# Linear attention: loads a group ahead and its two parts a group apart; two buffers for transposed cached keys

## The chip, the cores and the metric

The kernel runs on one core of a Trainium2 chip. The metric is the device time of one execution in microseconds. The instructions of each engine (PE is the matrix engine, DVE the vector engine, ACT the scalar engine, POOL is GpSimd, SP issues DMAs) form one list that the engine works off in order, and semaphores hold an instruction back until what it needs is there.

## What is computed

One layer of a decoder for 1024 prompt tokens and 8 sequences of 8 sample tokens (1088 rows). After an input projection, half of the mixing width is gated linear attention and half is latent attention, for the sample tokens over a paged cache of 8192 keys a sequence. Then come an output projection and a gated convolutional feed-forward net. The parts that matter here:

```python
def step(S, inp):                     # linear attention, one chunk of 64 tokens, 4 heads
    qc, kc, vc, gc = inp
    b = jnp.cumsum(gc, axis=1)
    o_inter = jnp.einsum('bchk,bhkv->bchv', qc * jnp.exp(b), S)
    diff = jnp.where(tri, b[:, :, None] - b[:, None, :], -jnp.inf)
    att = jnp.einsum('bthk,bshk,btshk->bhts', qc, kc, jnp.exp(diff))
    o_intra = jnp.einsum('bhts,bshv->bthv', att, vc)
    bl = b[:, -1]
    S_new = S * jnp.exp(bl)[..., None] + jnp.einsum('bshk,bshv->bhkv', kc * jnp.exp(bl[:, None] - b), vc)
    return S_new, o_inter + o_intra
...
s = jnp.einsum('bthl,bsl->bhts', ql, kv) + jnp.einsum('bthr,bsr->bhts', qr, kr)   # latent attention
p = jax.nn.softmax(jnp.where(k_pos[None, :] <= qp[:, None], s * scale, -jnp.inf))
return jnp.einsum('bhts,bsl->bthl', p, kv)
```

## The kernel before

All products are in fp32 (or in two rounded parts). The kernel is written in a tile framework: program text gives instructions and their rank, and a scheduler builds each engine's list from that rank, a modelled clock and the buffers that are free. Tiles live in pools; a tag with one buffer lets the next tile of that tag start only when every reader of the last one has finished, and a pool that is closed hands its space to the pool that follows with the same kind of waits.

After phase 1 (norm, input projection) two generators run side by side, `interleave` choosing by the work that each `yield` reports. One is `mla_sample`: for 8 sequences and 4 pieces of 2048 keys each it gathers rows (`L`, `R`) with POOL's indirect DMAs, transposes them on PE into `kps` (L1176), copies them with ACT into `KT` and `KR` (L1178), takes scores `S` (L1186, L1188), a running softmax (L1191 to L1215) and sums `O` (L1220). `KT` and `KR` have one buffer each; `kps` has two. Its rank is set 450 behind the other's, so it fills what the other leaves free.

The other, `main`, goes through the prompt's queries, `gla` (linear attention), `mla_prompt` (the prompt's latent attention) and the loads of the output weights. `gla` takes five groups: 4 is the sample tokens, 0 to 3 are 256 prompt tokens each. `gla_group` does one group from loads to store. Its first part depends on no other group: loads of `qT`, `kT`, `v`, `la` (L609 to L615), running sums `bps` and `bT` (L620, L623), seven levels of scores `lps` written into `att` (L630 to L679; each level is e on POOL and DVE, its exponential on ACT, products `Ab` and `Bb` on DVE, 16 small matmuls), decayed queries and keys `qe`, `ek`, `ke`, `dec` (L683 to L700). Its second part carries the state `S`: four chunk steps of `ops` (L716, L723), `ups` (L808) and the update of `S` and `Sb` (L728 to L735), or `gla_sample` for group 4, then norm, gate (L746) and the store (L747). `v`, `la`, `bT`, `att`, `qe`, `ek`, `ke` and `dec` have one buffer. Group 4 has a pool of its own, "glas", which is closed before "gla" opens for the others:

```python
with self.pool("glas") as bp:
    yield from self.gla_group(G, cp, bp, pm, 4)
with self.pool("gla") as bp:
    for g in range(4):
        yield from self.gla_group(G, cp, bp, pm, g)
```

Of the kernel before, what the change touches and what calls it, by code (L numbers as in the profile page):

```python
# [10 lines left out]
F32 = mybir.dt.float32  # L11
# [4 lines left out]
ALU = mybir.AluOpType  # L16
AX = mybir.AxisListType
PSUM = bass.MemoryType.PSUM
DRAM = bass.MemoryType.DRAM

P = 128
# [18 lines left out]
def _consts():  # L40
    c = {}
    r = RO
# [22 lines left out]
    # the rows of a modulation: four parts of nine in steps of 32, then the bias  # L65
# [28 lines left out]
class Rows:  # L94
    """the transposes of all tokens' rows, in two parts each, by groups of tokens"""
# [10 lines left out]
class Kernel:  # L106
# [37 lines left out]
    def mm2(self, out, w, ws, start, stop):  # L144
        """sums over ws of products, 64 rows in w: their first parts, then their second ones; the sums of the
        result's two halves are what counts"""
        n = len(ws)
        for k in range(n):
            for j in range(2):
                self.nc.tensor.matmul(out, w[:, k], ws[k][j], start=start and k + j == 0, stop=stop and k + j == n)  # L150

    def halves(self, pool, ps, tag="rt", bufs=2):
        """the sums of rows r and 64 + r"""
        o = pool.tile([P, T if tag == "big" else D], F32, name=tag, tag=tag, bufs=bufs)[0:64, 0:ps.shape[1]]
        self.nc.vector.tensor_copy(o, ps[64:P])
        self.nc.vector.tensor_tensor(o, ps[0:64], o, ALU.add)
        return o

    def rstd(self, pool, ms, n, tag="rstd", ms2=None):
        p = ms.shape[0]  # L160
        t = pool.tile([P, n], F32, name=tag + "e", tag=tag + "e")
        r = pool.tile([P, n], F32, name=tag, tag=tag)
# [72 lines left out]
    def ada_section(self, sec, wp, pp, bufs, evac, rp=None):  # L235
# [9 lines left out]
                # four products side by side  # L245
# [60 lines left out]
    def gate(self, k, gvec, gp, name, gb):  # L306
        """gate rows times the norm's gain, for prompt and sample tokens: [128, 2, 1024]"""
# [18 lines left out]
    def to_T(self, xp, pp, xn, h, i, slot, nraw=3, eng=None, both=None):  # L326
        """xn: the normalized rows of tile i; their transposes, modulated, into h"""
# [24 lines left out]
    def phase1(self):  # L352
# [3 lines left out]
        with ExitStack() as es:  # L356
# [37 lines left out]
            # the sample tokens' two parts side by side  # L394
# [22 lines left out]
            def gates():  # L417
                """the forget gates"""
# [18 lines left out]
            def ada():  # L437
                """the other parts of the modulation, a little after each of the products"""
# [19 lines left out]
            # low-rank gate input and query latent  # L458
# [20 lines left out]
            # latents and rotary keys  # L479
# [24 lines left out]
            # GLA queries and keys, transposed  # L504
# [19 lines left out]
            # indices of the sixteenths of pages, by partition  # L524
# [8 lines left out]
            # values and output gates  # L533
# [18 lines left out]
    def rope(self, xp, out, x, tab, h):  # L552
        """out, x: [n, h, 64]; tab [n, 2, 64]"""
# [13 lines left out]
    def gla(self):  # L567
        nc, A = self.nc, self.A
        with ExitStack() as es:
# [26 lines left out]
    def gla_group(self, G, cp, bp, pm, g):  # L596
        nc, A = self.nc, self.A
        sample = g == 4
        t0 = g * 256
        n = 64 if sample else 256  # L600
        nt = 1 if sample else 2
        nch = n // 64
        m = min(n, P)
        blk = 8 if sample else 64
        fl = lambda x: x[:, 0:2 * n].rearrange("p (a t) -> p a t", a=2)
        flat = lambda name, bufs=1: fl(bp.tile([P, 2 * n], F32, name=name, tag=name, bufs=bufs))
        rows = lambda name, bufs=1: bp.tile([P, nt, 512], F32, name=name, tag=name, bufs=bufs)[0:m]
        qT, kT = flat("qT", 2), flat("kT", 2)
        nc.sync.dma_start(qT, self.s_qk[0:2, :, t0:t0 + n].rearrange("c p t -> p c t"))  # L609
        nc.sync.dma_start(kT, self.s_qk[2:4, :, t0:t0 + n].rearrange("c p t -> p c t"))  # L610
# [14 lines left out]
        # intra-block scores, by levels  # L625
        # odd blocks of 64 on the upper partitions, where their values are
        npar, rows_ = (1, 64) if sample else (2, P)
        att = bp.tile([P, 2 * nt, P], F32, name="att", tag="att")[0:rows_]
        nc.gpsimd.memset(att, 0.0)
        for li, L in enumerate(LEVELS):  # L630
# [11 lines left out]
            else:  # L642
                G.flip ^= 1
                X = 2 * n // (2 * L)
# [3 lines left out]
                ref = b2[:, :, L - 1:L].broadcast_to([P, X, L])  # L648
# [44 lines left out]
        dec = bp.tile([P, 16], F32, name="dec", tag="dec")[:, 0:2 * nb].rearrange("p (a c) -> p a c", a=2)  # L693
# [5 lines left out]
        ke = bp.tile([P, nt, 2, P], F32, name="ke", tag="ke")[0:m]  # L699
# [3 lines left out]
        o_sb = rows("o_sb")  # L703
# [39 lines left out]
        rg = rows("rg")  # L743
        nc.sync.dma_start(rg, self.s_r[t0:t0 + n].rearrange("(i p) d -> p i d", p=m))
        self.head_norm(bp, o_sb, m, nt * 4)
# [4 lines left out]
    def head_norm(self, bp, o, m, nh, gg=None):  # L750
# [3 lines left out]
        sq = bp.tile([P, nh, P], F32, name="hsq", tag="hsq", bufs=1)[0:m]  # L754
# [3 lines left out]
        rs = self.rstd(bp, ms, nh, "hrs")  # L758
# [4 lines left out]
    def gla_sample(self, cp, pm, qe, ke, dec, v, at2, o_sb):  # L763
# [17 lines left out]
        for b in range(8):  # L781
            Sb = Sbs[b % 2]
            for h in range(2):
                hr = slice(64 * h, 64 * h + 64)
                nc.scalar.copy(Sb[hr, :, h], Sall[hr, b])
# [5 lines left out]
            self.outer(ups, lambda p, h: km[:, b, p * P + 64 * h:p * P + 64 * h + 64], v[:, 0])  # L791
            nc.gpsimd.tensor_tensor(Sall[:, b], Sall[:, b], dec[:, :, b:b + 1].broadcast_to([P, 2, P]), ALU.mult)
            nc.vector.tensor_tensor(Sall[:, b], ups, Sall[:, b], ALU.add)
            nc.sync.dma_start(A["o_gla_s"][0, b].rearrange("(p h) k v -> (h k) p v", h=2), Sall[:, b])
# [8 lines left out]
    def outer(self, out, k, v):  # L803
        """the heads' sums of keys times values, two heads side by side"""
# [15 lines left out]
    def mla_weights(self, mp, pp):  # L820
# [5 lines left out]
        # the first head's first  # L826
# [77 lines left out]
    def sample_queries(self, zs, xs, ds, es2):  # L904
        """the sample tokens' queries, and the prompt's last ones"""
# [24 lines left out]
            # the last tokens: those of the prompt, then the sample tokens  # L930
# [23 lines left out]
    def prompt_queries(self):  # L954
        """the prompt's other queries, and the attention among the new tokens"""
# [13 lines left out]
    def mix(self, gen, side, ratio, chain=None):  # L969
        """run gen, and side by its side in proportion, and a step of chain after each of gen's; what gen returns"""  # L970
# [12 lines left out]
    def mla_prompt(self):  # L983
        nc, A = self.nc, self.A
        with ExitStack() as es:
# [23 lines left out]
            def split2(x, name):  # L1009
                """both parts of [128, 2, n]"""  # L1010
# [6 lines left out]
            def keys(h):  # L1017
                """a head's keys, transposed"""
# [14 lines left out]
            def vals(pr):  # L1033
                """a pair of heads' values"""
# [14 lines left out]
            def scores(h, m):  # L1049
# [3 lines left out]
                # the rotary queries, twice: their first parts, then their second ones  # L1053
# [43 lines left out]
            def values(h, m, ps_, ls):  # L1097
# [3 lines left out]
                for j0 in range(0, end, 2):  # L1101
                    # the last block is the second tile's only
# [622 lines left out]
```

## Time and profile before

| what | us |
|---|---|
| median of three runs | 1891.44 (1888.42 to 1892.9) |
| span of the profiled execution | 1894.2 |
| PE busy in it | 1815.7 (96%) |
| DVE, ACT, POOL busy in it | 939.5, 709.2, 527.4 |

The profiled execution is one of its own, recorded by its span alone, from the first to the last instruction. Linear attention runs from about 400 to 640 us of the span, beside pieces of the sample attention, which itself lasts from about 333 to 960 us. Busy shares are of the span. A PE that is busy may still run at half of its clock; PEclk, the granted clock, says when.

### The profile page before, as it was taken

The page shows a single profiled execution, that of the slowest core. Times are in us where ns is not written, and L with a number is a line of the kernel's source. Part 1 is how long each engine was busy: PE and PEld are TensorE (multiplying, and loading weights), DVE is VectorE, ACT ScalarE, POOL GpSimd, SP SyncE. Part 2 cuts the span into 40 slices and gives each one's busy share as a digit, 9 for nine tenths or more (in the row PEclk, how much of TensorE's full clock was granted, in tenths as well). Part 3 has the DMA queues.
Part 4 walks back from the last instruction along what each step waited for, and adds up shares of the span by engine and source line. Part 5 has one row for each costly group of instructions (what it writes and reads, how often), then busy time and mean ns, then how long its engine had stood idle before and what let it go on. Part 6 is the DMA issues. An engine that isn't in the chain of part 4 may idle for free.

```text
span 1894.2 us, 30775 instructions
## 1 busy us (share of the span) xinstructions
PE 1815.7 (96%) x12403; PEld 1502.5 (79%) x12403; DVE 939.5 (50%) x1680; ACT 709.2 (37%) x1398; POOL 527.4 (28%) x567
## 2 busy tenths in 40 slices
PE   6999999998998899999999999999999999999998
PEld 3888767764555567776679999999999999888787
DVE  4740334355676445554557755555555554623433
ACT  3451112464456556756633422222222222323322
POOL 2640101243334323232102123333333332202221
PEclk8999999999989999999999999999999999999999
DMA  8155553565454744545445331111121212744563
GB/s 312 68 171 180 187 160 111 192 206 180 169 183 159 250 160 150 188 138 180 159 145 176 101 98 68 61 64 63 68 70 69 70 62 70 246 115 114 155 188 94
DMA packets 170617, 265.26 MB, mean 140 GB/s; under 512 B 18277, under 2 KB 118693, under 8 KB 162282
## 3 DMA queue, kind: packets, MB, share of 16 engines
q1 hardware_dynamic: 156138, 179.39, 29.6%
q0 software_dynamic: 14336, 83.89, 12.7%
q8 instruction: 98, 1.61, 0.3%
q14 instruction: 45, 0.37, 0.1%
HBM read 221.49 MB, written 41.75 MB: 139 GB/s over the span
## 4 chain that ended last, share of the span: by engine, by line
PE 83%; DVE 6%; DMA 5%; ACT 3%; issue 2%; POOL 1%; SPq 1%; DVEq 0%; POOLq 0%; ACTq 0%
PE ups L140 9%; PE ups L142 9%; PE ups L141 9%; PE kps L1176 6%; PE yps L142 4%; PE yps L140 4%; PE yps L141 4%; PE zps L140 3%; PE O L1220 3%; PE zps L142 3%; PE zps L141 3%; PE S L1186 3%; PE y L142 2%; PE y L140 2%; PE y L141 2%
## 5 line engine op out<-in xcount | busy, mean ns | idle before, releaser
L140 PE MATMUL ups<-gh,uhi 128*128 128x384 f32 (+1 forms) x1056 | 347.2, 329 | 0.3 <-DVE hraw L343 0.3
L141 PE MATMUL ups<-gl,uhi 128*128 128x384 f32 (+1 forms) x1056 | 346.7, 328 | 0.0
L142 PE MATMUL ups<-gh,ulo 128*128 128x384 f32 (+1 forms) x1056 | 346.5, 328 | 0.0
L1514 DVE TENSOR_SCALAR cv<-u,vt 128x1024 f32<-128x1024 f32 (+1 forms) x88 | 133.2, 1534 | 216.3 <-ACT u L1504 179.4
L140 PEld LDWEIGHTS ups<-gh,uhi 128*128 128x128 f32 x1056 | 198.3, 188 | 0.7 <-DVE hraw L343 0.6
L142 PEld LDWEIGHTS ups<-gh,ulo 128*128 128x128 f32 x1056 | 198.3, 188 | 0.1
L141 PEld LDWEIGHTS ups<-gl,uhi 128*128 128x128 f32 x1056 | 198.3, 188 | 0.0
L1176 PE MATMUL kps<-ident,L 128*128 128x128 f32 x1024 | 159.9, 286 | 22.4 <-ACT KT L1178 16.2
L1178 ACT COPY KT<-kps 128x512 f32<-128x512 f32 x256 | 145.8, 590 | 82.8 <-PE kps L1176 77.5
L1176 PEld LDWEIGHTS kps<-ident,L 128*128 128x128 f32 x1024 | 113.8, 143 | 78.8 <-issue 42.5
L121 POOL TENSOR_TENSOR ulo<-uraw,uhi 128x2048 fp32r<-128x2048 f32 x24 | 111.4, 4642 | 207.5 <-ACT uhi L1342 204.6
L1504 ACT COPY u<-ups 128x384 f32<-128x384 f32 (+1 forms) x130 | 57.6, 444 | 279.2 <-PE ups L142 279.2
L142 PE MATMUL yps<-uhi,gl 128*128 128x512 f32 x341 | 133.3, 392 | 5.0 <-DVE gl L121 5.0
L140 PE MATMUL yps<-uhi,gh 128*128 128x512 f32 x341 | 133.1, 391 | 0.0
L141 PE MATMUL yps<-ulo,gh 128*128 128x512 f32 x341 | 133.0, 390 | 0.0
L121 DVE TENSOR_TENSOR gl<-graw,gh 128x1408 fp32r<-128x1408 f32 x31 | 59.1, 1908 | 129.3 <-ACT gh L1561 129.3
L1167 POOL DMA_INDIRECT R<-cache_krope,idx x64 | 66.1, 1033 | 181.6 <-PE kps L1176 148.5
L1342 ACT CAST uhi<-uraw 128x2048 fp32r<-128x2048 f32 (+1 forms) x38 | 70.8, 1865 | 94.4 <-PE ups L141 66.9
L1561 ACT CAST gh<-graw 128x1408 fp32r<-128x1408 f32 (+1 forms) x35 | 45.8, 1310 | 158.1 <-PE yps L141 128.6
L1166 POOL DMA_INDIRECT L<-cache_latent,idx x64 | 61.5, 961 | 138.9 <-PE O L1220 68.4
L140 PE MATMUL zps<-whi,hh 128*128 128x512 f32 (+2 forms) x256 | 96.1, 375 | 0.0
L142 PE MATMUL zps<-whi,hl 128*128 128x512 f32 (+2 forms) x256 | 94.2, 368 | 0.8 <-DVE hl L121 0.8
(443 smaller groups left out, 3799.1 us busy)
## 6 DMA issues: line engine op xcount, KB each, us to landing
wraw<-w_ada SPq DMA_DIRECT2D x48, 512.0 KB
uraw<-w_ffn_up SPq DMA_DIRECT2D x22, 1024.0 KB
graw<-s_g SPq DMA_DIRECT2D x32, 704.0 KB
s_g<-gl SPq DMA_DIRECT2D x22, 544.0 KB
uraw<-w_ffn_down SPq DMA_DIRECT2D x10, 1024.0 KB
xt<-x_prompt SPq DMA_DIRECT2D x16, 512.0 KB
wraw<-w_in SPq DMA_DIRECT2D x12, 512.0 KB
uraw<-w_o SPq DMA_DIRECT2D x4, 1024.0 KB
```

What stands on the lines that cost most here:

```text
L121: eng.tensor_tensor(out, x, hi.bitcast(F32), ALU.subtract)
L140: mm(out, wh, xh, start=start, stop=False)
L141: mm(out, wh, xl, start=False, stop=False)
L142: mm(out, wl, xh, start=False, stop=stop)
L1166: nc.gpsimd.indirect_dma_start(L.rearrange("p j l -> p (j l)"), None, cl, io)
L1167: nc.gpsimd.indirect_dma_start(R.rearrange("p j l -> p (j l)"), None, ck, io)
L1176: nc.tensor.transpose(ps[:, k], x, self.ident)
L1178: nc.scalar.copy(KT[:, q // 2, j0:j0 + 4] if q < 4 else KR[:, 4 * half:4 * half + 4], ps)
L1186: nc.tensor.matmul(S[r], Q[:, c], KT[:, c, :, r], start=(c == 0), stop=False)
L1342: self.nc.scalar.copy(hi, raw)
L1504: copy(u[:, 2 + c0:2 + c0 + m], ps[:, 0:m])
L1514: nc.vector.tensor_scalar(yv[z], sh(2)[z], self.cw2[:, ch:ch + 1], self.cb[:, ch:ch + 1], ALU.mult, ALU.add)
```

## The change

`gla_group` is cut in three. `gla_load` allocates and loads `qT`, `kT` and `la`, and is called one group ahead of the first part. `gla_intra` is the first part, `gla_inter` the second. A group's `gla_inter` runs next to the following group's `gla_intra` through `beside`, which picks by work done as `interleave` does. Both pools are open together: "gla" holds everything that groups share, sized for the prompt's groups, "glas" only what the sample group needs. `v`, `la`, `att`, `qe`, `ke` and `dec` get two buffers. In `gla_sample` the masked keys are made one sequence at a time (three buffers in place of eight parts), the states are loaded four ahead into five buffers in place of eight, and there is a `yield` after each sequence in place of one for all. `KT` and `KR` get two buffers. Comments are dropped throughout.

```diff
-            with self.pool("glas") as bp:
-                yield from self.gla_group(G, cp, bp, pm, 4)
-            with self.pool("gla") as bp:
-                for g in range(4):
-                    yield from self.gla_group(G, cp, bp, pm, g)
+            bp = es.enter_context(self.pool("gla"))
+            order = (4, 0, 1, 2, 3)
+            with self.pool("glas") as sp:
+                ahead = self.gla_load(bp, 4)
+                for n, g in enumerate(order):
+                    X, ahead = ahead, self.gla_load(bp, order[n + 1]) if n < 4 else None
+                    intra = self.gla_intra(G, bp, pm, X)
+                    if n == 0:
+                        yield from intra
+                    else:
+                        yield from self.beside((inter, 15.0 if n == 1 else 11.4), (intra, 10.3))
+                    if n == 1:
+                        break
+                    inter = self.gla_inter(G, bp, sp, pm, X)
+            for n in (2, 3, 4):
+                inter = self.gla_inter(G, bp, None, pm, X)
+                X, ahead = ahead, self.gla_load(bp, order[n + 1]) if n < 4 else None
+                yield from self.beside((inter, 11.4), (self.gla_intra(G, bp, pm, X), 10.3))
+            yield from self.gla_inter(G, bp, None, pm, X)
+
+    def beside(self, *gens):
+        live = [[0.0, total, g] for g, total in gens]
+        while live:
+            it = min(live, key=lambda x: x[0] / x[1])
+            try:
+                c = next(it[2])
+                it[0] += c
+            except StopIteration:
+                live.remove(it)
+                continue
+            yield c
+
+    def gla_load(self, bp, g):
...
+        X.qT, X.kT = X.flat("qT", 2), X.flat("kT", 2)
+        nc.sync.dma_start(X.qT, self.s_qk[0:2, :, t0:t0 + n].rearrange("c p t -> p c t"))
+        nc.sync.dma_start(X.kT, self.s_qk[2:4, :, t0:t0 + n].rearrange("c p t -> p c t"))
+        X.la = bp.tile([P, 2, 256], F32, name="la", tag="la", bufs=2)[0:m, 0:nt]
+        nc.sync.dma_start(X.la, self.s_la[t0:t0 + n].rearrange("(i p) k -> p i k", p=m))
+        return X
+
+    def gla_intra(self, G, bp, pm, X):
...
-        v = rows("v")
+        X.v = v = X.rows("v", 2)
         nc.sync.dma_start(v, self.s_v[t0:t0 + n].rearrange("(i p) d -> p i d", p=m))
-        la = bp.tile([P, nt, 256], F32, name="la", tag="la")[0:m]
-        nc.sync.dma_start(la, self.s_la[t0:t0 + n].rearrange("(i p) k -> p i k", p=m))
...
-        att = bp.tile([P, 2 * nt, P], F32, name="att", tag="att")[0:rows_]
+        X.att = att = bp.tile([P, 4, P], F32, name="att", tag="att", bufs=2)[0:rows_, 0:2 * nt]
...
-        qe = flat("qe")
+        X.qe = qe = flat("qe", 2)
...
+    def gla_inter(self, G, bp, sp, pm, X):
...
-            self.gla_sample(bp, pm, qe, ke, dec, v, att, o_sb)
-            yield 15.0
+            yield from self.gla_sample(sp, pm, qe, ke, dec, v, att, o_sb)
...
-        km = cp.tile([64, 8, 256], F32, name="km")
-        for b in range(8):
-            nc.scalar.mul(km[:, b], ke[:, 0].rearrange("p a k -> p (a k)"), self.small[0:64, 96 + b:97 + b])
...
-        Sall = cp.tile([P, 8, 2, P], F32, name="Sall")
-        for b in range(8):
-            nc.sync.dma_start(Sall[:, b], A["state_gla"][0, b].rearrange("(p h) k v -> (h k) p v", h=2))
+        def load(b):
+            Ss.append(cp.tile([P, 2, P], F32, name="Sall", tag="Sall", bufs=5))
+            nc.sync.dma_start(Ss[b], A["state_gla"][0, b].rearrange("(p h) k v -> (h k) p v", h=2))
+        for b in range(4):
+            load(b)
...
+            if b < 4:
+                load(b + 4)
+            km = cp.tile([64, 256], F32, name="km", tag="km", bufs=3)
+            nc.scalar.mul(km, ke[:, 0].rearrange("p a k -> p (a k)"), self.small[0:64, 96 + b:97 + b])
...
+            yield 1.8
...
-                        KT = bp.tile([P, 2, 16, P], F32, name="KT", tag="KT", bufs=1)
-                        KR = bp.tile([P, 8, P], F32, name="KR", tag="KR", bufs=1)
+                        KT = bp.tile([P, 2, 16, P], F32, name="KT", tag="KT", bufs=2)
+                        KR = bp.tile([P, 8, P], F32, name="KR", tag="KR", bufs=2)
```

## Rows read from the trace of the kernel before

**Rows 1.** The page: PE's busy tenths and granted clock in 40 slices of 47 us.

```profile
PE   6999999998998899999999999999999999999998
...
PEclk8999999999989999999999999999999999999999
```

**Rows 2.** Windows by stage: busy us (instructions) by engine, granted clock, DMA share, GB/s.

```profile
330.00:400.00 70.00, 66.53 (x571) 50.87 (x570) 25.76 (x87) 32.66 (x67) 21.07 (x20) 1.00 0.53 191
400.00:640.00 240.00, 213.70 (x2224) 133.32 (x2228) 149.02 (x382) 134.69 (x292) 95.64 (x105) 0.95 0.55 185
640.00:960.00 320.00, 306.90 (x2627) 214.24 (x2616) 165.89 (x474) 194.12 (x468) 81.91 (x107) 0.99 0.51 170
...
1060.00:1620.00 560.00, 559.65 (x3457) 556.53 (x3456) 301.34 (x335) 140.68 (x239) 179.92 (x180) 1.00 0.21 73
```

**Rows 3.** Windows of 20 us in linear attention, columns PE, PEld, DVE, ACT, POOL, clock.

```profile
440.00:460.00 20.00, 12.68 (x135) 8.14 (x128) 7.58 (x20) 6.53 (x13) 4.77 (x6) 0.84 0.71 253
...
500.00:520.00 20.00, 18.07 (x203) 12.43 (x206) 12.89 (x37) 9.20 (x20) 5.41 (x7) 0.83 0.38 110
...
540.00:560.00 20.00, 16.93 (x184) 12.35 (x182) 16.22 (x37) 8.66 (x17) 6.22 (x6) 0.74 0.26 83
...
580.00:600.00 20.00, 15.98 (x183) 9.73 (x181) 19.62 (x44) 13.13 (x28) 11.54 (x12) 1.00 0.44 145
```

**Rows 4.** Waits of PE, 400 to 640 us: total us, times, longest.

```profile
PE kps L1176 <- ACT KT L1178: 11.1, 11, 7.0
PE lps L669 <- DVE Bb L662: 8.4, 5, 3.1
```

**Rows 5.** Timeline of the first prompt group's start: start us, duration, instruction.

```profile
437.87 0.37 SPq L609 DMA_DIRECT2D qT<-s_qk  x1
...
454.25 0.88 DVE L641 COPY B<-qT 64x512 f32<-64x512 f32 x2 [8.65 <-DMA qT<-s_qk]
...
456.83 1.11 PE L1176 MATMUL kps<-ident,L 128*128 128x128 f32 x4 [6.99 <-ACT KT L1178]
```

**Rows 6.** Waits of POOL, 400 to 640 us.

```profile
POOL att L629 <- PE ops L716: 20.4, 3, 8.4
```

**Rows 7.** Timeline of the second prompt group's start.

```profile
498.15 2.35 POOL L746 TENSOR_TENSOR o_sb<-o_sb,rg 128x1024 f32<-128x1024 f32 x1 [1.77 <-DVE o_sb L759]
498.51 2.27 DVE L650 TENSOR_TENSOR e<-bT 128x256 f32<-128x256 f32 x1
...
501.93 1.12 PE L669 MATMUL lps<-Bb,Ab 128*64 128x64 f32 x16 [2.70 <-DVE Bb L662]
```

**Rows 8.** Tile e, 400 to 640 us: duration in ns, shortest, median, longest.

```profile
L650 DVE TENSOR_TENSOR e<-bT x27: 229/424/2573, 406.6 to 596.2; 128x256 f32<-128x256 f32 x24, 128x64 f32<-128x64 f32 x3
```

**Rows 9.** Groups of POOL instructions, 400 to 640 us: busy us, mean ns.

```profile
L649 POOL TENSOR_TENSOR e<-bT 128x256 f32<-128x256 f32 (+1 forms) x27 | 17.5, 656 | 27.0 <-ACT KT L1178 10.1 <-DVE Bb L662 9.1 <-ACT bT L623 6.1
...
L746 POOL TENSOR_TENSOR o_sb<-o_sb,rg 128x1024 f32<-128x1024 f32 (+1 forms) x5 | 10.8, 2164 | 6.5 <-DVE o_sb L759 6.4
```

**Rows 10.** Waits of PE, 640 to 960 us.

```profile
PE kps L1176 <- ACT KT L1178: 4.2, 5, 2.3
```

**Rows 11.** Timeline: transposes of keys, four in a run and eight in a run.

```profile
495.17 0.66 PE L1176 MATMUL kps<-ident,L 128*128 128x128 f32 x4
...
498.15 1.09 PE L1176 MATMUL kps<-ident,L 128*128 128x128 f32 x8
```

**Rows 12.** Window of 5 us while the sample group loads.

```profile
405.00:410.00 5.00, 5.00 (x38) 2.58 (x38) 3.21 (x13) 4.17 (x13) 2.83 (x6) 1.00 0.98 350
```

**Rows 13.** Timeline of the end of the sample attention.

```profile
949.60 1.05 PE L1188 MATMUL S<-KR,Qd 128*32 128x256 f32 x16
...
953.25 0.91 SPq L1368 DMA_DIRECT2D mx<-s_mix  x2
```

**Rows 14.** Waits of ACT, 400 to 640 us.

```profile
ACT e L651 <- DVE e L650: 20.4, 10, 6.9
```

More of the change, by code (lines that the diff above doesn't have):

```diff
@@ L157, in halves, with rstd @@
         return o
-    def rstd(self, pool, ms, n, tag="rstd", ms2=None):
+    def rstd(self, pool, ms, n, tag="rstd", ms2=None, full=False):
         p = ms.shape[0]
-        t = pool.tile([P, n], F32, name=tag + "e", tag=tag + "e")
-        r = pool.tile([P, n], F32, name=tag, tag=tag)
+        t, r = (pool.tile([P, 8 if full else n], F32, name=x, tag=x)[:, 0:n] for x in (tag + "e", tag))
         if ms2 is None:
@@ L589, in gla @@
             G.flip = 0
-            with self.pool("glas") as bp:
-                yield from self.gla_group(G, cp, bp, pm, 4)
-            with self.pool("gla") as bp:
-                for g in range(4):
-                    yield from self.gla_group(G, cp, bp, pm, g)
[L596 to L601, printed above, removed]
+            bp = es.enter_context(self.pool("gla"))
@@ new lines, in gla_load @@
+    def gla_load(self, bp, g):
+        nc = self.nc
+        X = type("X", (), {})()
+        X.g, X.sample = g, g == 4
+        X.t0 = t0 = g * 256
+        X.n = n = 64 if X.sample else 256
+        X.nt = nt = 1 if X.sample else 2
+        X.m = m = min(n, P)
+        X.fl = lambda x: x[:, 0:2 * n].rearrange("p (a t) -> p a t", a=2)
+        X.flat = lambda name, bufs=1: X.fl(bp.tile([P, 512], F32, name=name, tag=name, bufs=bufs))
+        X.rows = lambda name, bufs=1: bp.tile([P, 2, 512], F32, name=name, tag=name, bufs=bufs)[0:m, 0:nt]
+        X.qT, X.kT = X.flat("qT", 2), X.flat("kT", 2)
[4 more added lines that the diff above has]
+        return X
@@ L602, in gla_group @@
+    def gla_intra(self, G, bp, pm, X):
+        nc = self.nc
+        sample, n, nt, m, t0, qT, kT, la, flat, fl = X.sample, X.n, X.nt, X.m, X.t0, X.qT, X.kT, X.la, X.flat, X.fl
         nch = n // 64
-        m = min(n, P)
         blk = 8 if sample else 64
-        fl = lambda x: x[:, 0:2 * n].rearrange("p (a t) -> p a t", a=2)
-        flat = lambda name, bufs=1: fl(bp.tile([P, 2 * n], F32, name=name, tag=name, bufs=bufs))
-        rows = lambda name, bufs=1: bp.tile([P, nt, 512], F32, name=name, tag=name, bufs=bufs)[0:m]
@@ L608, in gla_group @@
-        qT, kT = flat("qT", 2), flat("kT", 2)
-        nc.sync.dma_start(qT, self.s_qk[0:2, :, t0:t0 + n].rearrange("c p t -> p c t"))
-        nc.sync.dma_start(kT, self.s_qk[2:4, :, t0:t0 + n].rearrange("c p t -> p c t"))
-        v = rows("v")
+        X.v = v = X.rows("v", 2)
         nc.sync.dma_start(v, self.s_v[t0:t0 + n].rearrange("(i p) d -> p i d", p=m))
-        la = bp.tile([P, nt, 256], F32, name="la", tag="la")[0:m]
-        nc.sync.dma_start(la, self.s_la[t0:t0 + n].rearrange("(i p) k -> p i k", p=m))
@@ L643, in gla_group @@
                 G.flip ^= 1
-                X = 2 * n // (2 * L)
+                x2 = 2 * n // (2 * L)
                 Am = fl(Af)
@@ L647, in gla_group @@
                 e2 = flat("e", 2).rearrange("p a t -> p (a t)").rearrange("p (h x s) -> p h x s", h=2, s=L)
-                ref = b2[:, :, L - 1:L].broadcast_to([P, X, L])
+                ref = b2[:, :, L - 1:L].broadcast_to([P, x2, L])
                 nc.gpsimd.tensor_tensor(e2[:, 0], ref, b2[:, :, 0:L], ALU.subtract)
@@ L692, in gla_group @@
         nc.vector.tensor_tensor(ek, ek, kT, ALU.mult)
-        dec = bp.tile([P, 16], F32, name="dec", tag="dec")[:, 0:2 * nb].rearrange("p (a c) -> p a c", a=2)
+        X.dec = dec = bp.tile([P, 16], F32, name="dec", tag="dec", bufs=2)[:, 0:2 * nb].rearrange("p (a c) -> p a c", a=2)
         nc.scalar.activation(dec, bT.rearrange("p a (c t) -> p a c t", t=blk)[:, :, :, blk - 1], AF.Exp)
@@ L698, in gla_group @@
                 nc.tensor.transpose(kps[:, i, p], ek[:, p, i * P:i * P + m], self.ident)
-        ke = bp.tile([P, nt, 2, P], F32, name="ke", tag="ke")[0:m]
+        X.ke = ke = bp.tile([P, 2, 2, P], F32, name="ke", tag="ke", bufs=2)[0:m, 0:nt]
         nc.scalar.copy(ke, kps)
         yield 1.0
-        o_sb = rows("o_sb")
+    def gla_inter(self, G, bp, sp, pm, X):
+        nc, A = self.nc, self.A
+        g, sample, n, nt, m, t0 = X.g, X.sample, X.n, X.nt, X.m, X.t0
+        nch = n // 64
+        v, att, qe, ke, dec = X.v, X.att, X.qe, X.ke, X.dec
+        o_sb = X.rows("o_sb")
         if not sample:
@@ L739, in gla_group @@
         else:
-            self.gla_sample(bp, pm, qe, ke, dec, v, att, o_sb)
-            yield 15.0
-        rg = rows("rg")
+            yield from self.gla_sample(sp, pm, qe, ke, dec, v, att, o_sb)
+        rg = X.rows("rg")
         nc.sync.dma_start(rg, self.s_r[t0:t0 + n].rearrange("(i p) d -> p i d", p=m))
-        self.head_norm(bp, o_sb, m, nt * 4)
+        self.head_norm(bp, o_sb, m, nt * 4, full=True)
         nc.gpsimd.tensor_tensor(o_sb, o_sb, rg, ALU.mult)
@@ L748, in gla_group, with head_norm @@
         yield 0.2
-    def head_norm(self, bp, o, m, nh, gg=None):
+    def head_norm(self, bp, o, m, nh, gg=None, full=False):
         nc = self.nc
         o3 = o.rearrange("p i (h v) -> p (i h) v", v=P)
-        sq = bp.tile([P, nh, P], F32, name="hsq", tag="hsq", bufs=1)[0:m]
+        sq = bp.tile([P, 8 if full else nh, P], F32, name="hsq", tag="hsq", bufs=1)[0:m, 0:nh]
         ms = bp.tile([P, 8], F32, name="hms", tag="hms")[0:m, 0:nh]
@@ L757, in head_norm @@
         nc.vector.tensor_reduce(ms, sq, AX.X, ALU.add)
-        rs = self.rstd(bp, ms, nh, "hrs")
+        rs = self.rstd(bp, ms, nh, "hrs", full=full)
         nc.vector.tensor_tensor(o3, o3, rs.rearrange("p (h o) -> p h o", o=1).broadcast_to([m, nh, P]), ALU.mult)
@@ L782, in gla_sample @@
             Sb = Sbs[b % 2]
+            if b < 4:
+                load(b + 4)
+            km = cp.tile([64, 256], F32, name="km", tag="km", bufs=3)
+            nc.scalar.mul(km, ke[:, 0].rearrange("p a k -> p (a k)"), self.small[0:64, 96 + b:97 + b])
             for h in range(2):
                 hr = slice(64 * h, 64 * h + 64)
-                nc.scalar.copy(Sb[hr, :, h], Sall[hr, b])
+                nc.scalar.copy(Sb[hr, :, h], Ss[b][hr])
             r = slice(64 * (b % 2), 64 * (b % 2) + 64)
@@ L790, in gla_sample @@
             ups = pm.tile([P, 2, P], F32, name="ups", tag="M")
[L791 to L794, printed above, removed]
+            self.outer(ups, lambda p, h: km[:, p * P + 64 * h:p * P + 64 * h + 64], v[:, 0])
+            nc.gpsimd.tensor_tensor(Ss[b], Ss[b], dec[:, :, b:b + 1].broadcast_to([P, 2, P]), ALU.mult)
+            nc.vector.tensor_tensor(Ss[b], ups, Ss[b], ALU.add)
+            nc.sync.dma_start(A["o_gla_s"][0, b].rearrange("(p h) k v -> (h k) p v", h=2), Ss[b])
+            yield 1.8
         for p in range(2):
```

1 line of the change is left out of this document (added).

## The prediction

> **What bounds the kernel now.** The page comes first. PE is at nine tenths or more in every slice but five; three of the five lie between 426 and 663 us, and there is the one low granted clock behind the first slice, at 521 us [rows 1]. So this is a PE-bound program, and what can be won is time in which PE waits or runs at half its clock. The windows by stage say how much there is and where [rows 2]. From 1060 to 1620 us PE stands for 0.35 us in 560. From 640 to 960 us, where the sample attention runs beside the prompt's latent attention, it is idle for 320 - 306.9 = 13.1 us, and a clock of 0.99 costs another 306.9 x 0.01 = 3.1. From 400 to 640 us, where the sample attention runs beside linear attention, it is idle for 240 - 213.7 = 26.3 us. The clock's part of that stage is read from the three 20 us windows that carry it, busy time by the missing clock: 12.68 x 0.16 + 18.07 x 0.17 + 16.93 x 0.26 = 2.0 + 3.1 + 4.4 = 9.5 us [rows 3]. The stage thus loses 35.8 of its 240 us, 15%, against 16.2 of 320, 5%, in the stage behind it. PE's work at full clock in it is 213.7 - 9.5 = 204.2 us; DVE has 149 us there, ACT 135, POOL 96, so that none but PE is near a bound on average.
>
> The waits name two causes of the idle part: the transposes of keys waiting for ACT's copies, 11.1 us, and the level matmuls waiting for DVE's products, 8.4 us [rows 4]. The timeline shows what stands behind them. The first prompt group's qT load is issued at 437.87 us only, because "gla" opens on the space of "glas"; it lands for DVE at 454.25, ACT stands behind DVE's part of e with the copies of keys queued after it, and PE stands 6.99 us [rows 5]. This is the one load that comes late. The second kind is at each later group's start: the levels of a group come in one burst, after the last group's second part, since POOL's clearing of the single att waits for the last group's ops, 20.4 us in three times, and everything behind it on POOL waits too (the other parts of e, the gathers) [rows 6]. In the burst DVE is the bound: 19.62 of 20 us at 580 us, where PE loses 4.0 us [rows 3]. A pause of 2.70 us at 501.93 [rows 7] is followed by the lower clock.
>
> **The change, part by part.** Its sum is made against the profiled span of 1894.2 us and carried over to the median, 1891.4, which stands 2.8 lower.
>
> Removed: the hand-over of the pool. The next group's loads no longer need glas's space, and the first prompt group's first part runs beside the sample group's second part. The window from 440 us gives what goes: 20 - 12.68 = 7.3 idle and 2.0 of clock, 9.3 us [rows 3]. The next load that could be late is v, still loaded with the first part, but v is read by the second part alone, a group later.
>
> Moved: each group's levels next to the group before's chunk steps. The number of matmuls, products, exponentials and copies is the same, so the work at full clock stays 204.2 us. What remains of the loss I take from the nearest stage with two mixed streams: 16.2 us on 303.8 of work, 5.3%, gives 204.2 x 0.053 = 10.9. That would win 35.8 - 10.9 = 24.9 us, the first item's 9.3 included. Below it is bounded by nothing won besides the 9.3, above by all 35.8. I then give back 3 us: the sample group's first part and the last group's second part run without a partner, as now, and the gating product on POOL still falls beside the levels (below).
>
> The finer mix cuts PE's runs: eight transposes in one run take 1.09 us, two runs of four 1.32 [rows 11], so 0.23 a cut. The level matmuls come in 32 runs (seven levels in four groups, four in one); if each cut one more run, that is 7.4 us, if none, nothing. Most already stand between pieces, so I take 3.
>
> Loads: the first prompt group's qT, kT and la, 768 KB, now join the sample group's at 405 us, where the DMA engines are at 0.98 and move 350 GB/s [rows 12]: 2.2 us later for whatever queues behind them, on SP's list and among the gathers. If the sample group's own loads go first it costs nothing; I take 1. States loaded four ahead with five buffers make the fifth and later loads wait, on SP, for a store; each is needed four sequences later, with a first part beside it, so nothing is taken; without that cover a store's landing would cost some us once.
>
> KT and KR twice: a piece's copies need not wait for the last piece's scores. What it can win is at most what PE now waits for these copies where no load is to blame: 4.2 us from 640 to 960 us [rows 10] and the remaining 4.1 of rows 4. kps keeps two buffers, so ACT being late is not cured. I take 2, with bounds 0 and 8. The space it takes lies where phase 1's weights were, long read by then, and ahead of the output projection's tiles: their first load is issued at 953.25, after the last scores end at 950.65 [rows 13], so that is hidden now; uncovered it would be those two or three us.
>
> Sum: -24.9 + 3 + 3 + 1 - 2 = -19.9 us: **1891.4 - 19.9 = 1871.5, said as 1872.**
>
> One rule speaks against it. Row first: an e of DVE takes 2.27 us beside POOL's gating product of 2.35 us, where the median is 0.42 [rows 7, 8]. The Trainium skill (SBUF — State Buffer, Who interferes with whom) says that a DVE instruction with two SBUF inputs and a GpSimd instruction that reads SBUF lock each other out, the later one standing for the whole of the other. The trace agrees, and the rule asks more: mixed parts meet POOL more often. By it the time would be that of the second rival below.
>
> **The rivals.** *First, the sum above:* chance 0.62, own range 1859 to 1884 (gains of 32 to 8).
>
> *Second, only the hand-over goes.* DVE becomes the bound in the mix, held by POOL. POOL's e and gating products take 17.5 + 10.8 = 28.3 us [rows 9]; if DVE lost all of that anew, its 149 would be 177 of some 230 us, 77%, with bursts at 100% left at group starts. For it: 580 us as it is [rows 3]. Against: on average DVE then still has a quarter free, and the levels have a whole group's time in place of one burst. Time: 1891.4 - 9.3 + 4 (cuts and loads) = 1886. Chance 0.13.
>
> *Third, nothing.* The scheduler mixes across groups where buffers let it, and refills the gaps from the same lists; the hand-over's gap moves to another load, such as those at the start of the prompt's latent attention. 1889 to 1894, chance 0.11.
>
> *Fourth, slower: ACT becomes a convoy.* ACT works in order and serves both streams. It already waits 20.4 us for DVE's part of e, ten times [rows 14], and the copies of keys stand behind it; with both kps buffers full PE stops, whatever KT has. Today that happens in bursts. If the mix made every one of the 27 levels that take an exponential hold ACT 2 us, and PE had other work for 1 of them, PE would lose 27 us, and 20 won less 27 lost is +7: 1898. It decides from 0.74 us lost a level (20 / 27). Against: in a PE-bound mix DVE's part of e is ready long before ACT comes to it. Chance 0.14.
>
> **How the numbers follow.** The three runs spread by 4.5 us, 0.24%, so 0.2% is about what a measurement of this kernel can tell from no change. Faster by more: the first and second cases, 0.75. Same: the third, 0.11. Slower: the fourth, 0.14. The range runs from 1857, where all but an unlikely 34 us of loss is gone, to 1893, which takes in the second and third cases and leaves out the fourth and the thin end below, under 0.2 together.
>
> **What would show it.** Right: no PE pause of several us near the first prompt group's start, its qT load issued around 400 us; POOL's clearing of att no longer waiting for ops; PE's share in linear attention from 0.89 to about 0.95, its clock at 0.99 or 1.00 there; DVE's 20 us windows flat, near 14; the prompt's latent attention starting some 18 us earlier, and everything behind it moved by that much with the same lengths. Wrong: PE idle time of the stage still over 20 us; ACT's wait for DVE's e well over 20 us, with PE waiting for KT's copies; or the time won by 640 us lost again by 960, because the sample attention's pieces end last.

## The result, and the profile after

The changed kernel takes 1877.26 us (1875.51 to 1880.71, four runs) beside 1890.24 of the kernel before on the same chip (1888.42 to 1892.9, four runs): a ratio of 0.9935, 95% interval 0.9922 to 0.9949, or 13 us less. The forecast was 1872, faster by 19.9. The profiled execution has a span of 1876.1 us, 18.1 less than that of before. Spans stand some 1.8 us under the times here (1876.1 goes with 1877.96), so the execution that was profiled before was a long one, some 6 us above its median, and the one after 0.7 above its own: five of those 18 us are the choice of executions.

The page, busy tenths and granted clock by slices of 47 us, to set beside [rows 1]:

```profile
PE   6999999999998999998889999999999999999998
...
PEclk7999999999999999999989999999999999999999
```

Before, the slices under nine tenths, but for the first and the last, began at 426, 568 and 616 us, as the forecast read them, and the low clock stood at 521. Now one begins at 563, and three stand next to each other from 844 to 985 us, with the low clock in the last of them. The windows by stage [rows 2] and then the 20 us windows that matter [rows 3], columns PE, PEld, DVE, ACT, POOL, clock, DMA share, GB/s:

```profile
400.00:640.00 240.00, 225.14 (x2372) 144.79 (x2373) 155.49 (x403) 143.80 (x309) 99.62 (x108) 0.99 0.60 202
640.00:960.00 320.00, 299.84 (x2587) 215.29 (x2587) 166.65 (x465) 192.01 (x453) 79.63 (x105) 0.97 0.51 172
...
400.00:560.00 160.00, 156.09 (x1744) 99.50 (x1745) 123.90 (x312) 100.69 (x215) 75.33 (x84) 1.00 0.60 200
440.00:460.00 20.00, 20.00 (x231) 12.77 (x228) 13.54 (x28) 11.50 (x24) 10.87 (x13) 1.00 0.62 218
500.00:520.00 20.00, 18.29 (x216) 12.16 (x208) 19.02 (x39) 12.72 (x28) 12.32 (x11) 1.00 0.29 80
540.00:560.00 20.00, 20.00 (x196) 11.76 (x193) 9.95 (x23) 11.62 (x24) 8.31 (x7) 1.00 0.57 192
560.00:580.00 20.00, 16.44 (x168) 9.48 (x170) 8.69 (x28) 12.40 (x27) 10.15 (x8) 1.00 0.51 178
580.00:600.00 20.00, 14.24 (x106) 8.30 (x97) 5.77 (x18) 8.05 (x20) 3.91 (x5) 0.83 0.71 225
600.00:620.00 20.00, 18.37 (x178) 12.30 (x178) 7.55 (x22) 11.00 (x23) 5.95 (x7) 1.00 0.61 204
920.00:940.00 20.00, 12.56 (x133) 7.97 (x128) 14.49 (x32) 12.69 (x20) 0.94 (x2) 0.96 0.49 152
940.00:960.00 20.00, 17.05 (x129) 14.24 (x130) 6.13 (x9) 3.57 (x9) 0.00 (x0) 0.78 0.65 237
```

From 400 to 560 us, which now holds nearly all of linear attention, PE is idle for 3.9 of 160 us at a clock of 1.00. The loss that is left stands at two other places. From 560 to 620 us it is 60 - 49.05 = 10.95 idle and 14.24 x 0.17 = 2.4 of clock, 13.4 us. From 920 to 960 us it is 10.4 idle and 12.56 x 0.04 + 17.05 x 0.22 = 4.3 of clock, 14.6 us; before, these two windows lost 5.2 idle and 1.5 of clock.

What each stream did is read from the first and last start of its matmuls (count, shortest, median and longest duration in ns, then first to last start in us). Before, and then after:

```profile
L669 PE MATMUL lps<-Bb,Ab x396: 222/222/369, 409.9 to 604.0; 128*64 128x64 f32 x198
L142 PE MATMUL olps<-pth,vl x80: 272/281/287, 693.6 to 965.9; 128*128 128x256 f32 x64, 128*128 128x128 f32 x16
L1220 PE MATMUL O<-L,pt x1024: 379/379/637, 360.3 to 959.6; 128*32 128x256 f32 x171
L140 PE MATMUL y<-uhi,mh x256: 278/283/385, 967.7 to 1081.7; 128*128 128x256 f32 x128
```

```profile
L704 PE MATMUL lps<-Bb,Ab x396: 219/222/272, 407.9 to 540.9; 128*64 128x64 f32 x198
L142 PE MATMUL olps<-pth,vl x80: 273/281/416, 636.0 to 924.7; 128*128 128x256 f32 x64, 128*128 128x128 f32 x16
L1266 PE MATMUL O<-L,pt x1024: 378/379/637, 357.5 to 944.6; 128*32 128x256 f32 x171
L140 PE MATMUL y<-uhi,mh x256: 279/283/416, 948.2 to 1064.8; 128*128 128x256 f32 x128
```

The levels end 63 us earlier, the prompt's latent attention (olps) 41, the sample attention (O) 15, and the output projection (y) begins 19.5 earlier. Before, the two attentions ended 6 us apart, the prompt's last. Now the sample attention ends 20 us behind the prompt's, and for those 20 us it has PE to itself: a chain of scores, softmax and sums with gaps in it. The timeline of DVE and then of PE shows the last piece:

```profile
927.46 2.29 DVE L121 TENSOR_TENSOR ulo<-uraw,uhi 128x2048 fp32r<-128x2048 f32 x1
...
930.00 2.28 DVE L121 TENSOR_TENSOR ulo<-uraw,uhi 128x2048 fp32r<-128x2048 f32 x1
...
937.10 2.29 DVE L121 TENSOR_TENSOR ulo<-uraw,uhi 128x2048 fp32r<-128x2048 f32 x1 [0.79 <-ACT uhi L1388]
939.43 0.46 DVE L1247 TENSOR_SCALAR nm<-mg 32x1 f32<-32x1 f32 x3
```

```profile
941.58 3.64 PE L1266 MATMUL O<-L,pt 128*32 128x256 f32 x32 [7.24 <-DVE pt L1261]
```

The row maxima nm stand behind DVE's split of an output weight, PE waits 7.24 us, and then runs the 32 products of O at the lower clock (0.50 granted): 3.64 us. They take 1.93 at the full one (the last section shows both).

### The profile page after: what moved, and what is told of

Read it like the earlier page. It is cut to its first block, busy times and chain, and to the rows that moved or that the text cites. A ratio compares the mean times of both kernels' runs of the same rounds, so it can differ in the third digit from the quotient of the medians.

```text
span 1876.1 us, 30729 instructions
## 1 busy us (share of the span) xinstructions
PE 1803.9 (96%) x12403; PEld 1500.3 (80%) x12403; DVE 934.0 (50%) x1680; ACT 709.7 (38%) x1398; POOL 527.6 (28%) x567
## 4 chain that ended last, share of the span: by engine, by line
PE 84%; DMA 5%; DVE 5%; ACT 3%; issue 1%; POOL 1%; SPq 1%; DVEq 0%; POOLq 0%; ACTq 0%
PE ups L140 9%; PE ups L142 9%; PE ups L141 9%; PE kps L1222 6%; PE yps L142 4%; PE yps L141 4%; PE yps L140 4%; PE zps L140 4%; PE zps L141 3%; PE zps L142 3%; PE O L1266 3%; PE S L1232 3%; PE adaps L248 2%; PE y L140 2%; PE y L142 2%; PE y L141 2%
```

## The experiments

The runs of the kernel before that stand beside them had a median of 1895.4 us in the first group and 1895.3 in the third, 1889.8 in the second and 1890.2 with the result, a spread of 0.3%. The changed kernel itself was timed only where the kernel before took 1890 (1877.3 and 1877.2 us); its one-buffer copy stands in the first group (1878.3). Ratios are therefore compared within a group; across groups 0.003 is not read.

**First group: which part of the change counts.** KT and KR, back to one buffer in the changed kernel, and with two in the kernel before:

```diff
-KT = bp.tile([P, 2, 16, P], F32, name="KT", tag="KT", bufs=2)
+KT = bp.tile([P, 2, 16, P], F32, name="KT", tag="KT", bufs=1)
```

> The changed kernel with KT and KR back to one buffer each; nothing else. Theory (the time was won by the new order of linear attention, the second buffers are worth little): 1877 to 1879 us, ratio to the kernel before 0.993 to 0.995, PE waits for KT's copies by 1 to 2 us more over the sample attention. Rival (the second buffers brought a good part, up to the bound of 8 us): 1882 to 1886 us, ratio 0.996 to 0.998.

> The kernel before with two buffers for KT and KR; nothing else. Theory: 1887 to 1890 us, ratio 0.999 to 1.000 (the forecast's term was 2 us). Rival (the buffers bring the gain by themselves): 1880 to 1884 us, ratio 0.995 to 0.997.

Measured: 1878.29 us, ratio 0.9904 (0.9887 to 0.9922), and 1894.32, ratio 0.9995 (0.9984 to 1.0007). The spans with one buffer and with two are 1876.4 and 1876.1 us, and PE waits for KT's copies, 400 to 960 us, 6.7 us in place of 5.5. The engines' lists are the same with one and with two. The second buffers are worth nothing that can be measured; in the kernel before this is a comparison within the group, in the changed one it rests on the two spans.

The two parts of a group in sequence, everything else as changed:

```diff
-yield from self.beside((inter, 11.4), (self.gla_intra(G, bp, pm, X), 10.3))
+yield from inter
+yield from self.gla_intra(G, bp, pm, X)
```

> The changed kernel with each group's second part written ahead of the next group's first part in place of beside it; one pool, loads ahead and double buffers stay. Theory (the mix of levels and chunk steps is what keeps PE fed; the hand-over of the pool alone is 9.3 us of stage loss, of which the end of the sample attention takes half): 1882 to 1886 us, ratio 0.996 to 0.998, DVE above 19 us of 20 in one or more windows of linear attention. Rival (the hand-over and the early loads are all that counts, since two buffers let the scheduler run ahead by itself): 1876 to 1879 us, ratio 0.993 to 0.994.

Measured: 1900.41 us, ratio 1.0025 (1.0014 to 1.0037): slower than the kernel before, and 22 us slower than the one-buffer kernel beside it. Both numbers expected were too low, and DVE stays under the 19 us of 20 that the theory asked for. Its windows:

```profile
440.00:460.00 20.00, 18.03 (x219) 11.42 (x220) 18.51 (x37) 12.95 (x26) 11.36 (x13) 1.00 0.64 211
480.00:500.00 20.00, 14.31 (x130) 9.55 (x129) 17.88 (x41) 11.51 (x23) 9.66 (x9) 0.75 0.27 89
520.00:540.00 20.00, 15.99 (x142) 9.55 (x146) 13.26 (x28) 13.36 (x27) 11.56 (x10) 1.00 0.22 74
960.00:980.00 20.00, 8.66 (x45) 7.99 (x46) 11.34 (x13) 5.08 (x9) 0.93 (x2) 0.57 0.90 320
```

The gap of the hand-over is gone (18.03 at full clock from 440 us, where [rows 3] has 12.68 at 0.84), and the bursts of levels stay: PE waits 6.8 us for Bb, nine times, as against 8.4 [rows 4] and 1.3 in the changed kernel. In the stage from 400 to 640 us PE loses 21.4 idle and 5.4 of clock, 26.8 us where the kernel before loses 35.8, so within the stage 9 us are won, as much as the hand-over's term. They are lost again at the end: the levels end 11 us earlier than before, the sample attention only 1, and y begins at 974.5, because its rows mx are loaded late. SP issues that load at 965.85 us, right behind the store of the prompt attention's last rows at 965.43, and those rows stand on DVE behind two splits of output weights (DVE's line, then PE's):

```profile
958.49 4.50 DVE L121 TENSOR_TENSOR ulo<-uraw,uhi 128x2048 fp32r<-128x2048 f32 x2 [0.88 <-ACT uhi L1390]
...
957.07 1.93 PE L1268 MATMUL O<-L,pt 128*32 128x256 f32 x32
...
972.67 1.97 PE L1423 MATMUL tps<-ident,mx 128*128 128x128 f32 x8 [7.29 <-DMA mx<-s_mix]
```

The output weights' second parts from POOL in place of DVE:

```diff
-self.block(wo[:, :, 256 * q:256 * q + 256], nc.vector)
+self.block(wo[:, :, 256 * q:256 * q + 256], nc.gpsimd)
```

> The changed kernel with the second parts of the output weights taken by POOL in place of DVE (four subtractions). Theory (the last pieces of the sample attention stand behind DVE's three splits of 2.29 us each, and the end of that attention sets the start of the output projection): PE loses 4 to 6 us less from 920 to 960 us, 1872 to 1875 us, ratio 0.990 to 0.992. Rival one (the last softmax is a chain of its own that takes as long without the splits): 1876 to 1878 us, ratio as the changed kernel's. Rival two (a split takes POOL over 4 us, the first y waits for the weights): 1879 to 1884 us.

Measured: 1882.39 us, ratio 0.9931 (0.9915 to 0.9947), 4 us slower than the one-buffer kernel beside it. The second rival has the time, and the length of a split, twice what it takes DVE:

```profile
L121 POOL TENSOR_TENSOR ulo<-uraw,uhi x28: 4519/4608/5297, 893.6 to 1753.4; 128x2048 fp32r<-128x2048 f32 x28
```

Its wait was another, though: y does not wait for the weights but, 4.22 us, for the load of mx, which SP issues at 945.38 us, behind a load of the next weights at 944.97, and POOL's last split ends at 944.94. The last product of O starts at 944.8 us (945.0 in the one-buffer kernel) and y at 953.3 (949.6). With the splits off DVE the row maxima nm are complete 2.4 us earlier than in the one-buffer kernel (937.89 against 940.32), but then ACT makes its own part of an output weight ahead of the exponential p, which starts at 940.25 (940.44):

```profile
938.44 1.90 ACT L1388 CAST uhi<-uraw 128x2048 fp32r<-128x2048 f32 x1 [0.99 <-DMA uraw<-w_o]
940.25 0.68 ACT L1250 ACTIVATE p<-S,nm 128x512 f32<-128x512 f32 x1
```

So the split on DVE is not by itself what costs the end: where it goes, in this run the other half of a weight takes its place. What the last piece would take with neither of them in its way was not run.

**Second group: where the rest went.** `interleave` takes the generator that has done the smaller share of its total, so a smaller total for `main` has the sample attention written further ahead. The changed kernel again; then with the sample attention ahead in this way; with the store of linear attention's rows issued by POOL; with the loads not ahead:

```diff
-self.interleave((self.mla_sample(es2), 429.0, 450), (main(), 250.0, 0))
+self.interleave((self.mla_sample(es2), 429.0, 450), (main(), 230.0, 0))
...
-nc.sync.dma_start(self.s_mix[t0:t0 + n, 0:512].rearrange("(i p) d -> p i d", p=m), o_sb)
+nc.gpsimd.dma_start(self.s_mix[t0:t0 + n, 0:512].rearrange("(i p) d -> p i d", p=m), o_sb)
...
-X, ahead = ahead, self.gla_load(bp, order[n + 1]) if n < 4 else None
+X = self.gla_load(bp, order[n])
```

> The changed kernel itself, for the same chip as the three beside it: ratio to the kernel before 0.990 to 0.995 by every theory. If it comes out at 0.990, as the one-buffer kernel did, the second buffers of KT and KR are worth nothing; at 0.986 they would be worth what the forecast allowed.

> The changed kernel with main's total in the interleaving 230 in place of 250, so that the sample attention is taken further ahead and its last piece stands in PE's list before the last values of the prompt's attention, as in the kernel before; nothing else. Theory (part of what linear attention won is lost again because one piece of the sample attention stands alone at the end, where PE loses 14 us from 920 to 960 us): the loss there falls to some 5 us, ratio lower than the changed kernel's by 0.003 to 0.006. Rival (the sample attention's pieces were what filled PE elsewhere, so that the loss moves ahead, to the start of the prompt's latent attention): ratio within 0.001 of the changed kernel's.

> The changed kernel with the store of a group's rows into s_mix issued by POOL, which makes them, in place of SP; nothing else. Theory (the prompt attention's first loads stand on SP behind that store, 33 us at the longest, and land too late for PE at 560 to 600 us): the loads are issued some us earlier, PE's loss from 560 to 620 us falls from 13 to 5 to 8 us, ratio lower by 0.002 to 0.004 if the end of the sample attention lets it through, same if not. Rival (those loads wait for space that linear attention's tiles hold to their end, and SP's place in the list costs nothing): loads at the same time after the last product, ratio within 0.001 of the changed kernel's.

> The changed kernel with each group's qT, kT and la loaded when its own first part begins, not a group ahead; the pool, the two buffers and the parts beside each other stay. Theory (with a pool open and two buffers, SP gets to the loads early anyway, and what counts is the order of the parts): ratio within 0.001 of the changed kernel's. Rival (the loads a group ahead keep the levels fed): PE pauses of 3 us or more at each group's start, as the 6.99 us of the kernel before, 10 to 20 us in all, ratio 0.996 to 1.000.

Measured: changed again 1877.16 us, 0.9935 (0.9922 to 0.9948), by which the ratios of the two groups can't decide on the second buffers; the equal spans above speak against them. Sample attention ahead 1860.85 us, 0.9854 (0.984 to 0.9868), 16 us below it. Store from POOL 1871.47, 0.9907 (0.9892 to 0.9921). Loads with the first part 1871.29, 0.9905 (0.9892 to 0.9918).

The weight of 230 gave more than expected. Its windows at the two places, and its streams' ends:

```profile
560.00:580.00 20.00, 19.89 (x181) 11.05 (x174) 7.25 (x21) 12.68 (x26) 3.77 (x4) 1.00 0.63 228
580.00:600.00 20.00, 17.71 (x181) 10.53 (x178) 7.48 (x27) 11.45 (x28) 11.08 (x10) 1.00 0.67 228
600.00:620.00 20.00, 18.80 (x184) 11.53 (x186) 9.70 (x33) 12.54 (x29) 5.70 (x7) 1.00 0.84 304
900.00:920.00 20.00, 18.20 (x169) 11.50 (x168) 8.31 (x24) 7.93 (x18) 0.93 (x2) 0.91 0.27 87
```

```profile
L142 PE MATMUL olps<-pth,vl x80: 272/281/367, 647.6 to 921.3; 128*128 128x256 f32 x64, 128*128 128x128 f32 x16
L1266 PE MATMUL O<-L,pt x1024: 379/379/636, 359.2 to 917.7; 128*32 128x256 f32 x171
L140 PE MATMUL y<-uhi,mh x256: 278/283/583, 926.4 to 1045.1; 128*128 128x256 f32 x128
```

The two attentions end 4 us apart again, and the loss from 880 us to the first y falls from 19.6 us in the changed kernel beside it to 9.1. The loss at the start of the prompt's attention, 560 to 620 us, falls with it, from 13.7 to 3.6 us; the rival, which had it move there, is out. Added up over 20 us windows from 400 us to the first y, idle time and busy time by the missing clock, PE loses 41.0 + 12.7 us in the kernel before, 34.7 + 9.1 in the changed one, and 17.5 + 3.5 in this one.

The store from POOL lets SP issue the prompt attention's first loads earlier:

```profile
564.09 0.38 SPq L779 DMA_DIRECT2D o_gla_p<-S  x1
564.56 0.42 SPq L1040 DMA_DIRECT2D craw<-c_causal  x1
565.07 0.86 SPq L1047 DMA_DIRECT2D kvl<-s_kv  x2
```

In the changed kernel the store stands between:

```profile
560.29 0.38 SPq L779 DMA_DIRECT2D o_gla_p<-S  x1
572.69 0.36 SPq L787 DMA_DIRECT2D s_mix<-o_sb  x1
573.10 1.27 SPq L1040 DMA_DIRECT2D craw<-c_causal  x1
```

So SP stood 12 us there (the 33 us of the expectation was an earlier store). The loss from 560 to 620 us is 7.8 idle and 1.6 of clock, 9.4 us, in place of 13.7 in the changed kernel beside it. The ratio, lower by 0.003, is the theory's; the loss that is left is above its 5 to 8 us. The loads without their lead were expected to change nothing or to cost; they gained as much as the store. There the levels end at 550.6 us, 8 us later than in the changed kernel beside it, and PE stands less, 232.84 busy in 240 from 400 us as against 225.84; its work at full clock up to the first y is larger in turn, 514.0 us as against 505.3. So the loads a group ahead are not what feeds the levels; that they cost something is measured, by what way is not.

**Third group: is it the order of the parts, or the end?** The weight of 230 in the kernel before, in the sequence, with late loads, and with late loads and the store from POOL:

> The kernel before with main's total 230 in place of 250 in the interleaving; nothing else. Theory (there the sample attention and the prompt's attention already end within 6 us of each other, so that the weight only shifts work; what it gave the changed kernel, 0.008, was the time that the new order of linear attention had won and the end had lost): ratio 0.997 to 1.002. Rival (the weight is good by itself, whatever linear attention does): ratio 0.990 to 0.994.

> The changed kernel with the parts in sequence and main's total 230. Theory (the parts beside each other are worth some 20 us of PE in linear attention, wherever the sample attention ends): ratio 0.995 to 1.000, at least 0.010 above the kernel with the parts beside each other and 230. Rival (the sequence lost at the hand-over to the output projection alone, where 13.9 us lay between the sample attention's last product before its sums and the first y): ratio 0.985 to 0.990.

> The changed kernel with loads at the first part's beginning and main's total 230. Theory (loads a group ahead are not what feeds the levels, and in SP's list they stand ahead of others): ratio 0.982 to 0.986, at or a little under the kernel with 230 alone (0.9854). Rival (the late loads gained only because they moved the sample attention's end, which 230 moves too): ratio 0.986 to 0.989.

> The kernel beside it with the s_mix store of linear attention issued by POOL as well. Theory (each of the three gave time by itself, and the prompt attention's start still loses some us behind the store): ratio 0.979 to 0.983. Rival (the three mend the same loss, the end of the sample attention): ratio 0.983 to 0.987.

Measured: 1900.0 us, 1.0025 (1.0016 to 1.0034); 1892.74, 0.9999 (0.9986 to 1.0012); 1861.17, 0.9819 (0.9807 to 0.9832); 1870.46, 0.987 (0.9852 to 0.9889).

The weight is worth nothing to the kernel before; a little is lost, as y there begins at 974.0. The prompt's attention then ends 15 us behind the sample attention (972.3 against 957.4, where they lay 6 apart): the same number that brings the two ends together in the changed kernel takes them apart here. In the sequence y begins at 963.8 in place of 974.5; the ratio is lower by 0.0026, but across two groups, so it is not read as a gain. The order of the parts is still worth 32 us (1892.74 against 1861.17, late loads included). Late loads and 230 together give, within this group, the largest gain of all; in microseconds that is what 230 gave alone in its group (1860.85), so whether the two add is open. With the store from POOL besides, 9 us are lost again, against the expectation: each of these edits makes the scheduler write the lists anew, and they do not add. The same 9 us are the measure for how firmly the 16 us of the weight are tied to the ends of the two streams: the ends and the losses moved as that account says, in the changed kernel and the other way round in the kernel before, but 230 is the only other value that was tried.

## Why the prediction was right, and where not

**Right.** The hand-over went: the first prompt group's qT is issued at 399.50 us and the window from 440 us is full. The levels beside the chunk steps took away most of the burst: POOL's clearing of att waits 2.3 us for ops, not 20.4 [rows 6], and PE waits 1.3 us for Bb. ACT waits 11.3 us, eleven times, for DVE's e, not 20.4 [rows 14]: no convoy, the fourth rival is out.

```profile
PE lps L704 <- DVE Bb L697: 1.3, 3, 1.0
ACT e L686 <- DVE e L685: 11.3, 11, 2.6
```

One sign of being right did not come: DVE's 20 us windows are not flat near 14 but reach 18.7 to 19.0 in three of eight from 400 to 560 us. PE lost 1.7 us at the most in any of them, so the second rival, DVE as the bound, is out all the same. POOL's e takes 19.2 us and its gating products 11.0, against 17.5 and 10.8 in [rows 9], but no e of DVE takes 2.57 us any more [rows 8]:

```profile
L685 DVE TENSOR_TENSOR e<-bT x27: 220/444/849, 405.2 to 529.4; 128x256 f32<-128x256 f32 x24, 128x64 f32<-128x64 f32 x3
```

The prediction took from the rule of the Trainium skill (SBUF — State Buffer, Who interferes with whom), by which such instructions of DVE and POOL lock each other out, that mixed parts would meet POOL more often. On DVE this trace shows no price for it: the median of e went up by 20 ns, the longest one fell from 2573 to 849. POOL's e got longer, 783 ns in the median for 624; whether the lock did that is not shown.

**The step that failed is where the sum ended.** It summed the stage's loss up to 640 us and took everything behind it to move by as much with the same lengths. The stage's loss went from 35.8 us to 17.3, so -18.5 for -24.9: within linear attention's own 160 us 3.9 us are left, 2.4% where 5.3% was taken, and the other 13.4 came where the prompt's latent attention starts. Then main ran 41 to 63 us ahead of before and the sample attention only 15, with the weights of the interleaving left as they were, and the 14.6 us of loss at 920 to 960 us followed. From 880 us to the first y PE lost 19.8 us in place of 8.8. This was named among the signs of a wrong forecast, and had no term. That y nevertheless began 19.5 us earlier in the profiled executions, close to the sum, is luck: the 11 us lost at the end were made up by work that fell by 9.6 us, which had no term either (below). The weight of 230 shows its price: 16 us in the changed kernel, none in the kernel before.

**Terms.** Of KT's 2 us nothing was found. The 3 us given back for parts without a partner and for gating products did not come from 400 to 560 us, where all of the loss is 3.9, nor did the 1 us of loads at 405 us (PE is busy for 5.00 of 5.00 there, as in [rows 12]). The 3 us for cuts had the wrong sign: PE's work at full clock up to the first y, which the sum held fixed, is 567.7 - 53.7 = 514.0 us before and 548.2 - 43.8 = 504.4 after. Some 3 of these 10 are the start, which the profiled execution reached that much earlier (first O at 357.5, not 360.3). The levels are cut more, as forecast: counted in the trace, their products stand in 44 runs on PE, before in 27. What outweighs it is not settled. The scores from KR take 4.6 us less, in part because they are cut less, 37 runs for 44 (line groups, 330 to 970 us, busy us and mean ns; then timelines; each time before and after):

```profile
L1188 PE MATMUL S<-KR,Qd 128*32 128x256 f32 x512 | 40.9, 385 | 0.0
...
496.37 0.64 PE L1188 MATMUL S<-KR,Qd 128*32 128x256 f32 x8
...
497.58 0.64 PE L1188 MATMUL S<-KR,Qd 128*32 128x256 f32 x8
```

```profile
L1234 PE MATMUL S<-KR,Qd 128*32 128x256 f32 x512 | 36.3, 385 | 0.0
...
456.80 1.07 PE L1234 MATMUL S<-KR,Qd 128*32 128x256 f32 x16
```

**The hand-over as a gain of its own failed at the same step.** The second rival kept 9.3 us of it without the mix. The sequence had no hand-over, and its loss from 400 to 640 us was 9 us smaller than before. Its time was 5 us longer all the same: its levels ended 11 us earlier, its sample attention 1 us, and its output projection began 7 us later. For the change without its `beside`, the third rival (the gap moves to another load, here mx) comes nearest, and its range of 1889 to 1894 us, at most 1.0014, was still too low for 1.0025.

## What to carry to other kernels

When two streams share an engine and one of them is made faster, look where the other ends before the gain is summed: here 16 us, more than the change had brought, lay in one number of the interleaving that nobody had touched. Buffers, early loads and one pool together took no time off without the order (ratio 1.0025); with the order in which work was written next to other work, the kernel (its one-buffer copy, in the same group) was 22 us faster. Of the parts, KT's buffers and the early loads were taken out one by one, and neither was missed; the other buffers and the pool were not tried alone. And edits that each gain may not add when a scheduler writes the lists anew for each: the best version is measured, not summed.

## What the runs showed that was not expected

The clock makes a late chain dearer. After a wait of 7.24 us the 32 products of O took 3.64 us, and in the sequence, with 0.64 us idle two instructions ahead of them, 1.93. The granted clock of these stretches, the changed kernel's and then the sequence's, is 0.50 and 1.00, the two levels of 1.2 and 2.4 GHz:

```profile
941.60:945.20 3.60, 3.60 (x32) 1.37 (x32) 0.03 (x1) 0.00 (x0) 0.00 (x0) 0.50 1.07 391
...
957.07:959.00 1.93, 1.93 (x33) 0.94 (x32) 0.94 (x2) 1.93 (x2) 0.00 (x0) 1.00 0.93 261
```

A wait of 7 us cost 9. And sixteen score products of KR in one run took 1.07 us, eight and eight with other work between them 2 x 0.64 = 1.28.
